# Strassen sums of h by GpSimd, the first pair's first product among the direct blocks, a PSUM copy queued ahead of a split

## The chip, the cores and the metric

The kernel runs on one core of a Trainium2 chip. The metric is the time of one execution on the device in microseconds; several executions are timed, and their median counts. Engines are named as in the profile: PE (TensorE), with PEld for its weight loads, DVE (VectorE), ACT (ScalarE), POOL (GpSimd) and SP, which issues the DMAs. Each engine works through its own queue of instructions in order; semaphores tie the queues together.

## What is computed

One layer of a hybrid network on 1024 latent tokens of width 1024, with 256 context tokens as a prefix. A token mixer (state space scan, Fourier mixing and pooling side by side) is followed by a ConvFFN, and the change lies in the second:

```python
def conv_ffn(h, w_up, conv_w, conv_b, w_down, grid):
    a = h @ w_up
    a = dwconv2d_grid(a, conv_w, conv_b) if grid else dwconv1d(a, conv_w[1], conv_b)
    val, gate = jnp.split(a, 2, axis=-1)
    return (jax.nn.gelu(gate) * val) @ w_down
...
x = post_norm(x, mix_lat, g1, ln1_g[l], ln1_b[l])
ffn_lat = conv_ffn(modulate(x, sh2, sc2), ffn_w_up[l], ffn_conv_w[l], ffn_conv_b[l], ffn_w_down[l], True)
x = post_norm(x, ffn_lat, g2, ln2_g[l], ln2_b[l])
```

`w_up` has 2 x 2816 columns: 22 pairs of a value block and a gate block, 128 channels each. The convolution is a 3x3 depthwise one over a grid 64 tokens wide. All is float32.

## The kernel before

Numbers are split into a high and a low half (`hi = round(x)`, `lo = x - hi`, written to tiles of type float32r), and a product is three matmuls: high by high, high by low, low by high. `split` writes the high half on ACT and the low half on POOL unless another engine is given. The modulated input of the ConvFFN, h, lies transposed in `h2h[q]` and `h2l[q]`: q is the half of the tokens (512 each), and the middle index is one of eight blocks of 128 features.

The up-projection runs over the 22 pairs. The first seven (`PS = 7`) are direct: blocks n = 0 to 13, each 48 matmuls over eight feature blocks into a PSUM tile of 128 x 1024 (line 1521). After every second feature block `slot()` runs a unit of the down-projection (`down_unit`), if there is one: six matmuls into `pdn`, an eviction on DVE that adds them to `xt` (lines 1190 and 1192), and a store to `x_scratch`. There are two `pdn` buffers, and three tiles of 128 x 1024 in PSUM. After its matmuls a block is convolved by `conv2d`: one ACT instruction for the centre tap (line 1212) and eight DVE instructions for the others (line 1234), which read PSUM and add in SBUF. `gated` applies GELU on ACT, the product on POOL (line 1475) and the split. `down_raw` loads a block of `w_down` and scales it on POOL (line 1449).

The other 15 pairs use a Strassen scheme on part of the product: feature blocks `K2..K2+2` and `K1..K1+2` (2 to 4 and 5 to 7), the two halves of the tokens, and the value and gate columns make a 2 x 2 by 2 x 2 block product with seven multiplications. It needs sums of blocks on both sides:

- On the side of h they are made once, by `combine(k)` for k = 0, 1, 2, in pairs 3 to 5 (lines 1283 to 1300). `whole` adds the two halves of a block of h to one float32 block (four times, line 1288), four differences follow (lines 1295 to 1298), and three splits write `Tt`. All of it runs on DVE but for the high halves on ACT. The call stands in `tc.issue_after(lastv[0].ins)`: the instructions of the block that run on the engine of that last convolution tap, DVE, are ordered behind it. The buffers `ta` and the first half of `tb` are used by each k in turn. `last_t4` (line 1302) then writes a fourth group of sums into blocks `K1..K1+2` of `h2h[1]` and `h2l[1]`, once block 13 has read them.
- On the side of the weights they are made for each pair by `pair_sums` (lines 1317 to 1333), from the raw value and gate blocks that `pair_raw` loads into two buffers: sums and differences on POOL (1325, 1326, 1329, 1332), splits by ACT and POOL into the tiles S1, S2 and S3. These lie in the memory of `ta`, `tb` and `t4r`.

`pair(i)` (line 1372) runs the matmuls of one pair, all in `mm` (line 1349). `first_product(i)` is 9 matmuls of the value block by h into X, half of a PSUM tile, and ACT copies X to the other half Z (line 1370). Then X goes on with more products; Z gets those with S2 and S1, and a product with S3 goes to a tile `p7`. The first product of a later pair is issued at the end of the pair before it; that of pair 7 at the start of its own. `pair_value` splits the value block, `pair_gate` the gate block.

Tile, the layer that the kernel is written in, decides the order of the instructions in every engine's queue beforehand, by a list of what is ready in a model of the time, and by the order of writing where several are. So the order on chip can differ from that of the code; `tc.issue_after` adds edges. `eng = cycle(V)` gives DVE each time, `G` is POOL, `V` DVE, `S` ACT, `TE` PE.

Of the kernel before, what the change touches and what calls it, by code (L numbers as in the profile page):

```python
# [8 lines left out]
F32 = mybir.dt.float32  # L9
F32R = mybir.dt.float32r  # L10
AF = mybir.ActivationFunctionType
ALU = mybir.AluOpType
# [21 lines left out]
def hybrid_layer(  # L34
# [6 lines left out]
    V, S, G, TE = nc.vector, nc.scalar, nc.gpsimd, nc.tensor  # L41
# [22 lines left out]
    def psa(name):  # L64
        return psx[-1].tile([P, 1024], F32, tag="A", name=name, bufs=psx[1])
# [5 lines left out]
    def qt(tag, name, shape=(P, 1024), dt=F32):  # L71
        return qp.tile(list(shape), dt, tag=tag, name=name)
# [30 lines left out]
    for i, src in enumerate((c, c_ctx, ssd_conv_w, ssd_conv_b, ssd_norm_w, pool_scale, b_ada[:, 0:2048])):  # L103
# [4 lines left out]
        n = v.shape[0]  # L108
# [99 lines left out]
    def cycle(*items):  # L208
        st = [-1]

        def nxt():
            st[0] += 1
            return items[st[0] % len(items)]
        return nxt

    def split(raw, hi, lo, eng=None):

        S.activation(hi, raw, AF.Identity)  # L218
        return (eng or G).tensor_tensor(lo, raw, hi.bitcast(F32), op=ALU.subtract)  # L219
# [435 lines left out]
    def pre(n):  # L655
        return [lambda a=pres.pop(0): chunk_pre(*a) for _ in range(min(n, len(pres)))]
# [370 lines left out]
    rest = pre(16)  # L1027
# [60 lines left out]
    h2h, h2l = [None, None], [None, None]  # L1088
# [37 lines left out]
    KS, PS, TS = 3, 7, 3  # L1126
# [121 lines left out]
    def slot():  # L1248
        if units:
            down_unit(units.pop(0))  # L1250
# [27 lines left out]
    eng = cycle(V)  # L1278

    def t4raw(k):  # L1280
        return t4r[:, k, :] if k < 2 else tb[:, 1, :]

    def combine(k):

        ta, b22 = qt("q5", f"ta{k}", [P, 2, 512]), tb[:, 0, :]

        def whole(dst, q, kt):
            eng().tensor_tensor(dst, h2h[q][:, kt, :].bitcast(F32), h2l[q][:, kt, :].bitcast(F32), op=ALU.add)

        b11, b12, b21 = ta[:, 0, :], ta[:, 1, :], t4raw(k)  # L1290
        whole(b11, 0, K1 + k)
        whole(b12, 1, K1 + k)
        whole(b22, 1, K2 + k)
        whole(b21, 0, K2 + k)
        eng().tensor_tensor(b11, b12, b11, op=ALU.subtract)
        eng().tensor_tensor(b12, b22, b12, op=ALU.subtract)
        eng().tensor_tensor(b22, b22, b11, op=ALU.subtract)
        eng().tensor_tensor(b21, b21, b22, op=ALU.subtract)
        for j, src in ((0, b11), (1, b22), (2, b12)):
            split(src, Tt[j][k][:, 0, :], Tt[j][k][:, 1, :], eng())  # L1300
# [16 lines left out]
    def pair_sums(i):  # L1317


        v, g = raws[i]  # L1320
        s1, s2, s3 = [qt(tag, f"S{j}_{i}", [P, 8, P], F32R) for j, tag in enumerate(STAG)]
        sw[i] = {j: [(t[:, k, :], t[:, 3 + k, :]) for k in range(KS)] for j, t in ((1, s1), (2, s2), (3, s3))}
        sw[i][4] = [(s1[:, 6, :], s3[:, 6, :]), (s1[:, 7, :], s3[:, 7, :]), (s2[:, 6, :], s2[:, 7, :])]
        a11, a12, a21, a22 = v[:, K1 : K1 + KS, :], v[:, K2 : K2 + KS, :], g[:, K1 : K1 + KS, :], g[:, K2 : K2 + KS, :]
        G.tensor_tensor(a21, a21, a22, op=ALU.add)
        G.tensor_tensor(a11, a21, a11, op=ALU.subtract)
        split(a11, s2[:, 0:3, :], s2[:, 3:6, :])
        split(a21, s1[:, 0:3, :], s1[:, 3:6, :])
        G.tensor_tensor(a12, a12, a11, op=ALU.subtract)
        split(a12[:, 0:2, :], s1[:, 6:8, :], s3[:, 6:8, :])  # L1330
        split(a12[:, 2:3, :], s2[:, 6:7, :], s2[:, 7:8, :])
        G.tensor_tensor(a11, a22, a11, op=ALU.subtract)
        split(a11, s3[:, 0:3, :], s3[:, 3:6, :])

    def pair_gate(i):

# [15 lines left out]
    def wk(w, k0, n=KS):  # L1352
        return [(w[0][:, k, :], w[1][:, k, :]) for k in range(k0, k0 + n)]

    def sk(i, j):
        return sw[i][j]
# [7 lines left out]
    pv, pq, zc = {}, {}, {}  # L1364

    def first_product(i):
        pv[i] = psa(f"pu{chan[2 * i]}")
        X, Z = pv[i][:, 0:512], pv[i][:, 512:1024]
        mm(X, wk(vw[i], K1), hk(0, K1), True)
        zc[i] = S.copy(Z, X)  # L1370

    def pair(i, mid):

        more = i + 1 < NPAIR
        if i not in pv:
            first_product(i)
        X, Z = pv[i][:, 0:512], pv[i][:, 512:1024]
        mm(X, wk(vw[i], K2), hk(0, K2))
        mm(X, wk(vw[i], 0, KD0), hk(0, 0, KD0))
        if more:  # L1380
            slot()
        mm(Z, sk(i, 2), tk(2))
        pq[i] = psa(f"pu{chan[2 * i + 1]}")
        Y, W_ = pq[i][:, 0:512], pq[i][:, 512:1024]
        S.copy(Y, Z)
        if more:
            slot()
        p7 = psb(f"p7_{i}")
        mm(p7, sk(i, 3), tk(3), True)
        s7 = post.tile([P, 512], F32, tag="s7", name=f"s7_{i}")  # L1390
        s7c = S.copy(s7, p7)
        if more:
            with tc.issue_after(s7c.ins):
                pair_value(i + 1)
            slot()
        mm(Z, sk(i, 1), tk(1))
        seed = seedw[0] = S.copy(W_, Z)
        with tc.issue_after(seed.ins):
            mid()
            down_split()  # L1400
        slot()

        def z_end():
            mm(Z, sk(i, 4), hk(1, K2))
            mm(Z, wk(vw[i], 0, KD0), hk(1, 0, KD0))

        if more:
            mm(Y, wk(gw[i], K2), hk(1, K1))
            slot()
            z_end()  # L1410
            slot()
        else:
            z_end()
        acc_v = conv2d(pv[i], chan[2 * i], [(0, 16)], off=None if more else (ring("ht2", "cu0"), ring("ht2", "cd0")))
        if more:
            with tc.issue_after(tap[0].ins):
                pair_sums(i + 1)
            if i + 2 < NPAIR:
                pair_raw(i + 2, 0)
            first_product(i + 1)  # L1420
            slot()
        else:
            mm(Y, wk(gw[i], K2), hk(1, K1))
        mm(Y, wk(gw[i], 0, KD0), hk(0, 0, KD0))
        if more:
            slot()
        mm(W_, wk(gw[i], 0, KD0), hk(1, 0, KD0))
        if more:
            with tc.issue_after(zc[i + 1].ins):
                pair_gate(i + 1)  # L1430
            if i + 2 < NPAIR:
                pair_raw(i + 2, 1)
        pqv = pq[i][:].rearrange("p (a n) -> p a n", a=2)
        V.tensor_tensor(pqv, pqv, s7.unsqueeze(1).broadcast_to([P, 2, 512]), op=ALU.add)
        return acc_v
# [66 lines left out]
    for i in range(NPAIR):  # L1502
        if i < PS:
            for n in (2 * i, 2 * i + 1):
                if n > 1 and n + 1 < 2 * PS:
                    wu[n + 1] = up_weights(n + 1)
                if n == 2 * PS - 1:
                    pair_raw(PS, 0)
                    pair_raw(PS, 1)
                    pair_value(PS)  # L1510
                ct = chan[n]
                w = wu.pop(n)
                if n < 3:
                    pt = first[n]
                    up_half(pt, w, 0)
                else:
                    pt = psa(f"pu{ct}")
                    for k in range(KD):
                        for j, (a, b) in enumerate(((w[0], h2h), (w[0], h2l), (w[1], h2h))):
                            for q in range(2):  # L1520
                                TE.matmul(pt[:, q * 512 : q * 512 + 512], a[:, k, :], b[q][:, k, :],  # L1521
                                          start=k == 0 and j == 0, stop=k == KD - 1 and j == 2)
                        if k % 2 == 1:
                            slot()
                acc = conv2d(pt, ct, [(0, 9)], begun) if n == 0 else conv2d(pt, ct, [(0, 16)])
                if n % 2 == 0:
                    acc_v = acc
            down_split()
            between(i)
            if TS <= i < TS + KS:  # L1530
                with tc.issue_after(lastv[0].ins):
                    combine(i - TS)
            if i == PS - 1:
                last_t4()
                pair_sums(PS)
                pair_raw(PS + 1, 0)
                pair_gate(PS)
                pair_raw(PS + 1, 1)
        else:
            acc_v = pair(i, lambda: between(i))  # L1540
            if i < NPAIR - 1:
                acc = conv2d(pq[i], chan[2 * i + 1], [(0, 16)])
            else:
                acc = conv2d(pq[i], chan[2 * i + 1], [(0, 8), (8, 16)], off=(qt("q3", "cu1"), qt("wl0", "cd1")), early=True)
        accs_[i] = acc_v, acc
# [165 lines left out]
```

## Time and profile before

| | |
|---|---|
| median of 3 runs | 1211.18 us (1209.03 to 1214.26) |
| the profiled execution | 1215.51 us |
| its span, first to last instruction | 1213.7 us |
| busy, share of the span: PE | 1130.9 us, 93% |
| PEld | 918.5 us, 76% |
| DVE | 991.2 us, 82% |
| POOL | 590.2 us, 49% |
| ACT | 459.9 us, 38% |
| granted clock of TensorE, mean | 0.981 |

A row of a timeline has the start in us, the length in us, the engine, the line, the operation, what it writes and reads, and how many instructions are merged in it; brackets give the idle time of that engine before it and what ended it. A row of waits has the engine and line, what it waited for, and then the total in us, the times and the longest. The ConvFFN begins at about 466 us, its units of the down-projection at 546, its Strassen pairs at 685; after 1141 comes the end of the down-projection with the last normalisation.

### The profile page before, as it was taken

The numbers are of one execution on the slowest core, as the hardware profiler recorded it, in microseconds if no ns is written. First come the engines' busy times: TensorE is split into PE (matmuls) and PEld (weight loads), VectorE is DVE, ScalarE is ACT, GpSimd is POOL, SyncE is SP. The second block draws the span as 40 slices with busy tenths as digits, with TensorE's granted clock in tenths as the row PEclk, the third lists the DMA queues.
The fourth block names the chain that finished last, engine by engine and source line by source line (L and its number), as shares of the span: only waits on it lengthen the run. The fifth ranks groups of instructions, "written<-read, shape, count | busy, mean of one in ns | idle before, by whom it ended". The sixth has DMA issues, their size and how long they took to land.

```text
span 1213.7 us, 15187 instructions
## 1 busy us (share of the span) xinstructions
PE 1130.9 (93%) x5328; PEld 918.5 (76%) x5328; DVE 991.2 (82%) x1407; ACT 459.9 (38%) x790; POOL 590.2 (49%) x470
## 2 busy tenths in 40 slices
PE   4899998889878998999999989999999999999986
PEld 2698887768756887788777768888888888888864
DVE  4788787688899889798999956877887787878866
ACT  2263566621444133342231333333333434333553
POOL 0010122244254024573465386767676767676756
PEclk9999999999989999999999999999999999999988
DMA  9849475557525314214545445555555565555513
GB/s 314 282 154 321 139 202 169 158 195 234 183 78 192 119 48 163 89 58 141 167 157 160 125 151 185 181 186 187 191 191 186 178 191 191 191 187 187 186 48 139
DMA packets 151875, 206.48 MB, mean 170 GB/s; under 512 B 12253, under 2 KB 89067, under 8 KB 151799
## 3 DMA queue, kind: packets, MB, share of 16 engines
q1 hardware_dynamic: 151799, 205.51, 52.4%
q8 instruction: 42, 0.69, 0.2%
q14 instruction: 34, 0.28, 0.1%
HBM read 148.76 MB, written 56.71 MB: 169 GB/s over the span
## 4 chain that ended last, share of the span: by engine, by line
PE 58%; DVE 17%; DMA 11%; POOL 4%; ACT 4%; issue 4%; SPq 1%; DVEq 0%; POOLq 0%; ACTq 0%
PE pu L1349 20%; PE pdn L1187 13%; PE pu L1521 6%; PE pout L1010 4%; DMA bc<-cs_scratch 3%; PE pl L1576 3%; PE pz L344 2%; PE p L1349 2%; PE px L445 2%; DVE cv L1234 2%; PE pu L1245 1%; DMA wa<-in_w_ada_dram 1%; DMA ctxr<-in_ctx_dram 1%; DMA wdr<-in_ffn_w_down_dram 1%; ACT EU L645 1%
## 5 line engine op out<-in xcount | busy, mean ns | idle before, releaser
L1234 DVE SCALAR_TENSOR_TENSOR cv<-pu,ffc,cv 128x945 f32<-128x945 f32 (+6 forms) x362 | 425.6, 1180 | 74.6 <-ACT cv L1212 64.9
L1187 PE MATMUL pdn<-wd,gh 128*128 128x512 f32 x576 | 182.2, 397 | 6.6 <-DVE xt L1190 6.1
L1187 PEld LDWEIGHTS pdn<-wd,gh 128*128 128x128 f32 x576 | 108.4, 189 | 33.4 <-DVE xt L1190 7.8
L1190 DVE TENSOR_TENSOR xt<-xt,pdn 128x512 f32<-128x512 f32 x128 | 87.3, 682 | 33.3 <-PE pdn L1187 28.2
L1187 PE MATMUL pdn<-wd,gl 128*128 128x512 f32 x288 | 114.1, 396 | 0.0
L219 POOL TENSOR_TENSOR wul<-wur,wuh 128x1024 fp32r<-128x1024 f32 x29 | 71.6, 2469 | 57.3 <-ACT wuh L218 42.4
L1449 POOL TENSOR_TENSOR wdr<-wdr,g2b 128x512 f32<-128x512 f32 x44 | 57.4, 1308 | 61.5 <-DMA wdr<-in_ffn_w_down_dram 61.5
L219 POOL TENSOR_TENSOR S<-wur,S 128x384 fp32r<-128x384 f32 (+2 forms) x75 | 62.1, 854 | 31.3 <-ACT S L218 30.6
L1212 ACT ACTIVATE cv<-pu,ffc 128x1024 f32<-128x1024 f32 (+3 forms) x46 | 53.5, 1165 | 43.8 <-PE pu L1349 22.1
L1475 POOL TENSOR_TENSOR cv<-cv,cv 128x512 f32<-128x512 f32 x44 | 58.6, 1351 | 22.2 <-ACT cv L1474 22.2
L1349 PE MATMUL pu<-T,S 128*128 128x512 f32 x270 | 67.1, 392 | 0.0
L644 POOL TENSOR_TENSOR bc<-bc,ncs 128x256 f32<-128x256 f32 x32 | 25.8, 810 | 79.4 <-DMA bc<-cs_scratch 68.7
L1187 PEld LDWEIGHTS pdn<-wd,gl 128*128 128x128 f32 x288 | 54.4, 189 | 12.9
L1349 PE MATMUL pu<-h2h,wuh 128*128 128x512 f32 x150 | 59.9, 400 | 3.4 <-ACT pu L1370 3.4
L219 POOL TENSOR_TENSOR gl<-cv,gh 128x512 fp32r<-128x512 f32 x44 | 57.2, 1320 | 10.9 <-ACT gh L218 10.0
L1474 ACT ACTIVATE cv<-cv 128x512 f32<-128x512 f32 x44 | 25.5, 626 | 91.8 <-DVE cv L1234 91.8
L1349 PEld LDWEIGHTS pu<-T,S 128*128 128x128 f32 x270 | 50.7, 188 | 11.6
L1349 PE MATMUL pu<-h2h,wul 128*128 128x512 f32 x150 | 59.5, 396 | 0.0
L1349 PE MATMUL pu<-h2l,wuh 128*128 128x512 f32 x150 | 59.2, 395 | 0.0
L206 POOL TENSOR_TENSOR h2l<-h2t,h2h 128x512 fp32r<-128x512 f32 x14 | 20.6, 1478 | 77.6 <-DVE h2h L205 77.6
L219 POOL TENSOR_TENSOR wd<-wdr,wd 128x512 fp32r<-128x512 f32 x42 | 53.7, 1301 | 4.4 <-ACT wd L218 4.2
L1521 PE MATMUL pu<-h2h,wuh 128*128 128x512 f32 x176 | 55.6, 397 | 0.0
(407 smaller groups left out, 2923.5 us busy)
## 6 DMA issues: line engine op xcount, KB each, us to landing
xt<-x_scratch SPq DMA_DIRECT2D x144, 256.0 KB
x_scratch<-xt SPq DMA_DIRECT2D x144, 256.0 KB
wur<-in_ffn_w_up_dram SPq DMA_DIRECT2D x44, 512.0 KB
wad<-in_w_ada_dram SPq DMA_DIRECT2D x32, 512.0 KB
wdr<-in_ffn_w_down_dram SPq DMA_DIRECT2D x44, 256.0 KB
wa<-in_w_ada_dram SPq DMA_DIRECT2D x32, 256.0 KB
bc<-cs_scratch SPq DMA_DIRECT2D x32, 256.0 KB
xr<-in_x_dram SPq DMA_DIRECT2D x8, 512.0 KB
```

The lines of the kernel that those rows point to most:

```text
L219: return (eng or G).tensor_tensor(lo, raw, hi.bitcast(F32), op=ALU.subtract)
L644: G.tensor_tensor(bc[:, 1], bc[:, 1], ncs[:, ch, b : b + 2].unsqueeze(2).broadcast_to([P, 2, P]), op=ALU.add)
L1010: TE.matmul(pt[:, nb * 512 : nb * 512 + 512], u, v[:, nb * 512 : nb * 512 + 512], start=first and i == 0, stop=last and i == 2)
L1187: TE.matmul(pt, u_, wd[nb][:, v_, :], start=i == 0, stop=i == n - 1)
L1190: V.tensor_tensor(xt, xt, pt, op=ALU.add)
L1212: tap[0] = S.activation(acc[:, a * 64 : b * 64], pt[:, a * 64 : b * 64], AF.Identity, bias=ffc[:, 396 + ct : 397 + ct], scale=factor(0, 0))
L1234: last = V.scalar_tensor_tensor(dst, pv[:, r0 + dy : r1 + dy, c0 + dx : c1 + dx], factor(dy, dx), dst, op0=ALU.mult, op1=ALU.add)
L1349: TE.matmul(dst, a[k][u], b[k][w], start=start and k == 0 and j == 0, stop=k == n - 1 and j == 2, skip_group_check=True)
L1449: G.tensor_tensor(raw, raw, g2b[:, s], op=ALU.mult)
L1475: G.tensor_tensor(acc[:, s], acc[:, s], acc_v[:, s], op=ALU.mult)
L1521: TE.matmul(pt[:, q * 512 : q * 512 + 512], a[:, k, :], b[q][:, k, :], start=k == 0 and j == 0, stop=k == KD - 1 and j == 2)
L1576: TE.matmul(accs[t][nb], u_, wd[nb][:, v_, :], start=t < NHALF and m == 0 and i == 0, stop=m == NG - 1 and i == 2, skip_group_check=t >= N ...
```

## The change

```diff
@@ combine(k)
         def whole(dst, q, kt):
-            eng().tensor_tensor(dst, h2h[q][:, kt, :].bitcast(F32), h2l[q][:, kt, :].bitcast(F32), op=ALU.add)
+            G.tensor_tensor(dst, h2h[q][:, kt, :].bitcast(F32), h2l[q][:, kt, :].bitcast(F32), op=ALU.add)
@@ pair_sums(i)
         G.tensor_tensor(a21, a21, a22, op=ALU.add)
         G.tensor_tensor(a11, a21, a11, op=ALU.subtract)
+        G.tensor_tensor(a12, a12, a11, op=ALU.subtract)
         split(a11, s2[:, 0:3, :], s2[:, 3:6, :])
         split(a21, s1[:, 0:3, :], s1[:, 3:6, :])
-        G.tensor_tensor(a12, a12, a11, op=ALU.subtract)
         split(a12[:, 0:2, :], s1[:, 6:8, :], s3[:, 6:8, :])
         split(a12[:, 2:3, :], s2[:, 6:7, :], s2[:, 7:8, :])
-        G.tensor_tensor(a11, a22, a11, op=ALU.subtract)
-        split(a11, s3[:, 0:3, :], s3[:, 3:6, :])
+
+        def rest():
+            G.tensor_tensor(a11, a22, a11, op=ALU.subtract)
+            split(a11, s3[:, 0:3, :], s3[:, 3:6, :])
+
+        return rest
@@ pair(i, mid)
             with tc.issue_after(tap[0].ins):
-                pair_sums(i + 1)
+                rest = pair_sums(i + 1)
+            first_product(i + 1)
+            with tc.issue_after(zc[i + 1].ins):
+                rest()
             if i + 2 < NPAIR:
                 pair_raw(i + 2, 0)
-            first_product(i + 1)
             slot()
@@ the direct blocks
                         if k % 2 == 1:
                             slot()
+                        if k == 5 and n == 2 * PS - 1:
+                            first_product(PS)
@@ the end of the direct blocks
                 last_t4()
-                pair_sums(PS)
+                pair_sums(PS)()
                 pair_raw(PS + 1, 0)
```

Four things differ. The 12 sums of line 1288 go from DVE to POOL. In `pair_sums` the a12 difference is written ahead of the first two splits. The last difference and its split, into S3, become `rest`; from pair 8 on it is written after the first product of the pair and its PSUM copy `zc`, and its ACT instruction is ordered behind that copy, while for pair 7 it follows at once. And the first product of pair 7 is written inside block 13, after the sixth of its eight feature blocks and the unit there. The number of matmuls and of sums is the same.

## The prediction

> **What bounds the kernel now.** I read the busy time of each engine in stretches of 15 us first, then what TensorE waits for, then the engines' timelines around each wait, since a share over the whole span mixes stages.
>
> ```profile
> span 1213.7 us, 15187 instructions
> 665.00:680.00 15.00, 10.34 (x39) 8.24 (x38) 14.93 (x15) 3.74 (x7) 7.26 (x5) 0.89 0.31 98
> 710.00:725.00 15.00, 11.56 (x49) 9.08 (x48) 12.04 (x12) 5.55 (x11) 12.77 (x13) 0.98 0.34 105
> 740.00:755.00 15.00, 15.00 (x67) 12.18 (x66) 9.98 (x11) 5.20 (x11) 10.59 (x11) 1.00 0.42 141
> PE pdn L1187 <- DVE xt L1190: 6.1, 4, 4.7
> PE pu L1349 <- ACT pu L1370: 3.4, 1, 3.4
> ```
>
> The columns of a stretch are its bounds and length, then busy time of PE, PEld, DVE, ACT and POOL, the granted clock, the DMA share. PE is full from 740 on (15.00 of 15.00), so there only PE work counts. Before it stand two holes, both where the direct blocks hand over to the Strassen pairs, and both in code that the change touches. The two rows below the stretches (PE's waits from 500 to 740) name them: one wait of 4.7 us on an eviction by DVE, one of 3.4 us on the PSUM copy at L1370.
>
> The first hole, on PE, then DVE, then POOL:
>
> ```profile
> 662.16 0.63 PE L1521 MATMUL pu<-h2h,wuh 128*128 128x512 f32 x2
> 664.50 0.62 PE L1521 MATMUL pu<-h2h,wul 128*128 128x512 f32 x2
> 669.77 1.22 PE L1187 MATMUL pdn<-wd,gh 128*128 128x512 f32 x2 [4.66 <-DVE xt L1190]
> 675.59 0.62 PE L1187 MATMUL pdn<-wd,gh 128*128 128x512 f32 x2
> 660.07 2.91 DVE L1288 TENSOR_TENSOR ta<-h2h,h2l 128x512 f32<-128x512 f32 x2
> 662.91 3.47 DVE L1288 TENSOR_TENSOR tb<-h2h,h2l 128x512 f32<-128x512 f32 x2
> 666.30 2.82 DVE L1295 TENSOR_TENSOR ta<-ta 128x512 f32<-128x512 f32 x1
> 669.04 0.67 DVE L1190 TENSOR_TENSOR xt<-xt,pdn 128x512 f32<-128x512 f32 x1
> 674.27 0.68 DVE L219 TENSOR_TENSOR T<-ta,T 128x512 fp32r<-128x512 f32 x1
> 674.88 1.19 DVE L1234 SCALAR_TENSOR_TENSOR cv<-pu,ffc,cv 128x945 f32<-128x945 f32 x1
> 659.42 3.01 POOL L1449 TENSOR_TENSOR wdr<-wdr,g2b 128x512 f32<-128x512 f32 x2
> 662.39 3.43 POOL L1475 TENSOR_TENSOR cv<-cv,cv 128x512 f32<-128x512 f32 x2
> 665.79 2.79 POOL L219 TENSOR_TENSOR wul<-wur,wuh 128x1024 fp32r<-128x1024 f32 x1
> ```
>
> Ten matmuls lie between the starts 662.16 and 664.50: 0.234 us each. The next was due at 664.50 + 2 x 0.234 = 664.97 and came at 669.77: **4.80 us**. The 18 matmuls from there to 675.59 took 5.82 instead of 4.21, at a lower clock: **1.61 us** more. The hole costs 6.41 us. It is DVE's order: the eviction that PE needs stands behind five sums of combine(2). A sum takes 0.60 us from start to start when alone (674.27 to 674.88), but the four L1288 took 666.30 - 660.07 = 6.23 us and the L1295 2.74, just while POOL ran one two-input operation after another. Each of the two engines waits here for the other.
>
> The second hole, on PE, ACT, POOL:
>
> ```profile
> 719.74 0.40 PE L1349 MATMUL pu<-h2h,gwl 128*128 128x512 f32 x1
> 723.58 0.51 PE L1349 MATMUL pu<-h2h,wuh 128*128 128x512 f32 x1 [3.44 <-ACT pu L1370]
> 728.73 0.62 PE L1187 MATMUL pdn<-wd,gh 128*128 128x512 f32 x2
> 722.51 0.52 ACT L218 ACTIVATE S<-wur 128x384 fp32r<-128x384 f32 x1 [8.84 <-POOL wur L1332]
> 722.94 0.58 ACT L1370 COPY pu<-pu 128x512 f32<-128x512 f32 x1
> 717.17 1.30 POOL L1449 TENSOR_TENSOR wdr<-wdr,g2b 128x512 f32<-128x512 f32 x1 [1.56 <-DMA wdr<-in_ffn_w_down_dram]
> 718.43 3.09 POOL L219 TENSOR_TENSOR S<-wur,S 128x384 fp32r<-128x384 f32 x4
> 721.48 0.99 POOL L1332 TENSOR_TENSOR wur<-wur,wur 128x384 f32<-128x384 f32 x1
> 723.11 1.01 POOL L219 TENSOR_TENSOR S<-wur,S 128x384 fp32r<-128x384 f32 x1 [0.63 <-ACT S L218]
> ```
>
> Due at 719.97, PE went on at 723.58: 3.61 us; its next 15 matmuls took 5.15 instead of 3.51, 1.64 more. Together **5.25 us**. The copy itself (0.58) had nothing to wait for but its place in ACT's queue: the S split ahead of it waited 8.84 us for POOL's L1332, which stood behind four split halves, a multiply and that multiply's DMA.
>
> **The change part by part.**
>
> *Copy ahead of the last split.* The L1332 difference and its split come into rest(), and the split is queued on ACT behind the copy. Nothing is added. The copy then needs only the first product, which PE finished before the 12 gate matmuls that end at 719.97 and two units of six, 24 x 0.234 = 5.6 us earlier. So the 5.25 us go. What is late next: the second product of this pair reads S2, due 15 matmuls and one unit of six after 719.97, at 719.97 + 21 x 0.234 = 724.9; POOL has all four halves by 721.5, 3.4 us before. The third product reads S3, due 15 matmuls later, at 728.4; its low half ended at 724.12, 4.3 us before. POOL's chain moves with PE, since the GELU ahead of it is queued behind a PSUM copy. Gain **5.3**; least, if these two margins are eaten and more, 2. In the other 13 pairs PE has no hole; swapping two ACT steps of 0.5 us there costs nothing as long as these margins cover it, and 0.5 a pair if not. The earlier a12 difference on POOL changes nothing: it ran ahead of the splits already.
>
> *Sums on GpSimd.* DVE loses 12 sums, POOL gets 12. POOL's price, and the gaps that could take them:
>
> ```profile
> L219 POOL TENSOR_TENSOR wd<-wdr,wd 128x512 fp32r<-128x512 f32 x42 | 53.7, 1301 | 4.4 <-ACT wd L218 4.2
> 610.09 2.41 POOL L219 TENSOR_TENSOR wul<-wur,wuh 128x1024 fp32r<-128x1024 f32 x1 [14.75 <-PE pdn L1187]
> 644.93 2.41 POOL L219 TENSOR_TENSOR wul<-wur,wuh 128x1024 fp32r<-128x1024 f32 x1 [11.15 <-ACT wuh L218]
> 656.91 1.02 POOL L1325 TENSOR_TENSOR wur<-wur 128x384 f32<-128x384 f32 x1 [7.05 <-DMA wur<-in_ffn_w_up_dram]
> ```
>
> POOL pays 12 x 1.30 = 15.6 us, 5.2 a combine. The L1325 row tells where they will stand: it is written after block 13 (line 1535), yet runs at 656.91, before block 13's matmuls (662.16). The scheduler puts work of POOL where POOL is free. The edge on the last convolution tap binds DVE's instructions alone. combine(1) and combine(2) can sum as soon as the combine before has let go of its two buffers, and right there are POOL's gaps of 14.75 and 11.15 us; DVE then runs taps that read PSUM, at 1.2 us each (674.88, with POOL starting an operation beside it). So I cost them at nothing there; without that cover it is the slower rival below.
>
> What DVE saves in a combine is bounded both ways: 4 x 0.60 = 2.4 us if the waits on POOL pass to the seven operations that stay, 6.2 if they go. [...] For the third combine a start earlier by what DVE lags counts too:
>
> ```profile
> 644.75 1.19 ACT L1212 ACTIVATE cv<-pu,ffc 128x1024 f32<-128x1024 f32 x1
> 649.20 3.69 DVE L1234 SCALAR_TENSOR_TENSOR cv<-pu,ffc,cv 128x945 f32<-128x945 f32 x3
> ```
>
> Convolution 11 could start at 645.9 and starts at 649.20. Two combines shorter by at least 2.4 each take these 3.3 us away, so combine(2) starts 3.3 earlier. With all waits still in it the eviction then falls at 665.7 and PE resumes at 666.5: 1.5 us of hole and no long low clock, a gain of 4.9. Without the sums ahead of it the hole goes whole: 6.4. I take **5.6**, the middle, since wul and L1449 stay where they are. The other three evictions that PE waited for (6.1 - 4.7 = 1.4 us) are the same thing in small; I take half, **0.7**, between 0 and 1.4.
>
> One cost: sums of combine(0) that read only the second token half can start while DVE still works at the norms that hold up PE:
>
> ```profile
> 464.14 2.48 DVE L1080 SCALAR_TENSOR_TENSOR xa<-xa,pn_mv,ln1g 128x1024 f32<-128x1024 f32 x1
> 475.95 1.27 DVE L1080 SCALAR_TENSOR_TENSOR xa<-xa,pn_mv,ln1g 128x1024 f32<-128x1024 f32 x1
> ```
>
> A meeting with POOL costs such an operation 1.2 us, and two sums qualify: 0 to 2.4, I take **0.6**, half a meeting.
>
> *First product earlier.* Nine matmuls (2.1 us) move ahead of block 13's last 12; PE's work stays. But last_t4 may only overwrite h2h[1] after these 12, and S2 waits for last_t4:
>
> ```profile
> 683.49 0.62 PE L1521 MATMUL pu<-h2h,wul 128*128 128x512 f32 x2
> 686.29 0.62 ACT L218 ACTIVATE h2h<-tb 128x512 fp32r<-128x512 f32 x1
> 689.44 1.05 DVE L219 TENSOR_TENSOR h2l<-tb,h2h 128x512 fp32r<-128x512 f32 x1
> 692.32 2.25 PE L1349 MATMUL pu<-T,S 128*128 128x512 f32 x9
> ```
>
> From block 13's last matmuls to the product that reads S2 are 8.8 us now, 6.7 then. 2.5 us of the present chain are DVE's backlog (the h2l at 689.44 comes that long after its h2h ends); that shrinks as DVE gets ahead. Bounds 0 and 2.1; I take **1.0**, as ends this far apart have no row nearer to one.
>
> **Sum:** 5.3 + 5.6 + 0.7 - 0.6 - 1.0 = 10.0 us off. Against the profiled execution (1215.51 us, span 1213.7 and 1.8 around it) that is 1205.5; the median shown is 4.3 us lower, 1211.18, and the forecast from it is **1201**. From 740 on nothing absorbs it, as PE is full.
>
> **Rivals.**
>
> *One hole stays* (the eviction keeps its place behind all seven operations, or the copy's hole returns as a wait on S2 or S3). For it: POOL is 12.77 of 15 us busy around 715. Against: the margins of 3.4 and 4.3 us. Gain 3.5 to 7, about 1206.
>
> *Returned at the handover:* the S2 chain keeps its 8 us, PE arrives there 6 us sooner plus 2.1, and the gain of the first hole comes back as a wait there, with S3 behind it late as well. For it: DVE's order in that place is fixed beforehand. Against: the rest of the chain starts from PE's own matmuls, and DVE's part shrinks with its backlog. Gain 0 to 4, about 1209.
>
> *POOL's queue in front of DVE (slower):* the sums stand where they stood, behind L1449 and L1475. They then begin at 665.79 and end 5.2 later, at 671.0; DVE, whose L1295 began at 666.30, stands 4.7 us longer, with evictions and taps queued behind it. Three combines: 14.1, less 5.3, is 8.8 slower: 1220. It decides from the point where two combines sum after their convolution's last tap. [...]
>
> **How the numbers follow.** Forecast 0.56; one hole stays 0.22; returned 0.10; POOL's queue 0.12. A measurement of this kernel tells about 0.5% (6.1 us, 1205.1) from no change. Half of the second case lies beyond it: faster 0.56 + 0.11 = 0.67. Same: 0.11 + 0.10 + 0.02 of the last (one combine only) = 0.23; slower 0.10. The range begins at the best ends (6.4 + 1.4 + 5.3 = 13.1, so 1198) less 1.5 for the spread of runs, 1196.5; it takes in the second case and most of the third: up to 1210.
>
> **What would show it.** PE's waits: no L1370 row and no eviction over 2 us near 665; L1288 rows on POOL in its gaps around 600 and 635, at 1.3 us; convolution 11 starting within 1.5 us of its ACT step; any wait ahead of the first T,S product under 2 us. Wrong, if L1288 rows on POOL start after a convolution's last tap with DVE idle at L1295, if PE waits there for S, or if PE has new holes after 740.

## The result and the profile after

| | before | changed |
|---|---|---|
| median | 1210.66 us (4 runs, 1209.03 to 1214.26) | 1202.12 us (4 runs, 1199.98 to 1204.77) |
| ratio to before, 95% interval | | 0.9923 [0.9896, 0.9950] |
| the profiled execution, its span | 1215.51, 1213.7 us | 1204.77, 1202.9 us |
| granted clock of TensorE, mean | 0.981 | 0.981 |

The kernel became 8.5 us faster by the medians; the forecast was 1201 us. One run of the kernel before that took 3799.59 us stands in the median of the last batch below (1212.91 us, 11 runs), but not in its ratios. The page of the changed kernel, its span:

```profile
span 1202.9 us, 15202 instructions
```

The same stretches as before, with the same columns (bounds, length, busy time of PE, PEld, DVE, ACT, POOL, granted clock, DMA share, GB/s):

```profile
665.00:680.00 15.00, 14.66 (x64) 11.49 (x63) 14.86 (x15) 3.02 (x6) 4.86 (x4) 1.00 0.33 102
...
710.00:725.00 15.00, 14.57 (x64) 11.55 (x63) 13.16 (x14) 3.86 (x6) 10.89 (x11) 1.00 0.56 185
725.00:740.00 15.00, 15.00 (x67) 12.23 (x66) 10.22 (x12) 5.81 (x10) 10.53 (x9) 1.00 0.67 218
```

And what PE waits for from 500 to 750, whole:

```profile
PE p L1353 <- DVE xt L1190: 0.4, 1, 0.4
PE pu L1353 <- POOL S L219: 0.4, 1, 0.4
PE pdn L1187 <- DVE xt L1190: 0.3, 1, 0.3
PE pu L1245 <- DVE h2l L206: 0.2, 1, 0.2
```

PE is now busy 14.66 us of the 15 in which it had 10.34, at the full clock (1.00, where it had 0.89), and the two rows of 4.7 and 3.4 us are gone; nothing of half a microsecond has taken their place. After 740 PE's waits are the same in both kernels, 4.9 and 0.8 us at `pl`, so no new hole came there. Lines of the code moved a little: L1349 of before is L1353, L1370 is L1374, L1332 is L1334, L1475 is L1481, L1521 is L1527.

Where the first hole was, timeline of the changed kernel on ACT, DVE, POOL and PE:

```profile
644.92 1.19 ACT L1212 ACTIVATE cv<-pu,ffc 128x1024 f32<-128x1024 f32 x1
646.41 3.69 DVE L1234 SCALAR_TENSOR_TENSOR cv<-pu,ffc,cv 128x945 f32<-128x945 f32 x3
657.29 1.07 DVE L1295 TENSOR_TENSOR ta<-ta 128x512 f32<-128x512 f32 x1
658.35 0.69 DVE L1190 TENSOR_TENSOR xt<-xt,pdn 128x512 f32<-128x512 f32 x1
658.96 1.12 DVE L1296 TENSOR_TENSOR ta<-tb,ta 128x512 f32<-128x512 f32 x1
...
663.40 2.90 DVE L219 TENSOR_TENSOR T<-ta,T 128x512 fp32r<-128x512 f32 x1
...
669.07 0.68 DVE L1190 TENSOR_TENSOR xt<-xt,pdn 128x512 f32<-128x512 f32 x1
662.89 2.86 POOL L219 TENSOR_TENSOR wul<-wur,wuh 128x1024 fp32r<-128x1024 f32 x1
630.92 1.70 POOL L1288 TENSOR_TENSOR ta<-h2h,h2l 128x512 f32<-128x512 f32 x1 [1.23 <-DVE T L219]
635.40 1.30 POOL L1288 TENSOR_TENSOR ta<-h2h,h2l 128x512 f32<-128x512 f32 x1
636.67 1.31 POOL L1288 TENSOR_TENSOR tb<-h2h,h2l 128x512 f32<-128x512 f32 x1
669.80 0.72 PE L1187 MATMUL pdn<-wd,gh 128*128 128x512 f32 x2 [0.34 <-DVE xt L1190]
```

Four things are to be seen. Three of the four sums of combine(2) ran on POOL between 631 and 638, 19 us ahead of its differences. Convolution 11 starts 1.49 us after its step on ACT, 4.45 before. The waits of DVE on POOL are still there: the split at 663.40 takes 2.90 us beside POOL's `wul`, where the one at 674.27 before took 0.68, and the seven operations that are left take from 657.29 to 669.07. The eviction between L1295 and L1296 stands behind one operation of the combine instead of five. The next one came three operations later before; now it stands behind all the other six, 10.1 us from 658.96 to 669.07, and PE waits 0.34 us for it.

Where the second hole was, timeline of the changed kernel on ACT, POOL and PE:

```profile
708.55 0.57 ACT L1374 COPY pu<-pu 128x512 f32<-128x512 f32 x1 [0.73 <-PE pu L1353]
717.49 0.53 ACT L218 ACTIVATE S<-wur 128x384 fp32r<-128x384 f32 x1 [8.36 <-POOL wur L1334]
716.43 1.02 POOL L1334 TENSOR_TENSOR wur<-wur,wur 128x384 f32<-128x384 f32 x1
713.68 0.39 PE L1353 MATMUL pu<-h2h,gwl 128*128 128x512 f32 x1
713.91 0.39 PE L1353 MATMUL pu<-h2h,wuh 128*128 128x512 f32 x1
```

The copy now waits for PE alone, 5 us before it is needed. The split that stood ahead of it waits for POOL as long as ever, 8.36 us, with nothing of PE behind it.

### The profile page after: what moved, and what is told of

It is laid out like the page before. It is cut to its first block, busy times and chain, and to the rows that moved or that the text cites. A ratio compares the mean times of both kernels' runs of the same rounds, so it can differ in the third digit from the quotient of the medians.

```text
span 1202.9 us, 15202 instructions
## 1 busy us (share of the span) xinstructions
PE 1129.9 (94%) x5328; PEld 918.1 (76%) x5328; DVE 984.6 (82%) x1395; ACT 461.1 (38%) x790; POOL 609.5 (51%) x482
## 4 chain that ended last, share of the span: by engine, by line
PE 69%; DVE 16%; DMA 6%; issue 3%; ACT 3%; POOL 2%; SPq 0%; DVEq 0%; ACTq 0%; POOLq 0%
PE pu L1353 22%; PE pdn L1187 16%; PE pu L1527 9%; PE pout L1010 4%; PE px L445 4%; PE pz L344 4%; PE pl L1584 3%; PE p L1353 3%; DMA bc<-cs_scratch 2%; DVE cv L1234 1%; PE pu L1245 1%; POOL cv L1224 1%; DMA xr<-in_x_dram 1%; DMA zb_r<-in_w_in_dram 1%; PE pm L298 1%
## 5 line engine op out<-in xcount | busy, mean ns | idle before, releaser
L1481 POOL TENSOR_TENSOR cv<-cv,cv 128x512 f32<-128x512 f32 x44 | 57.9, 1336 | 27.7 <-ACT cv L1480 27.7
L1353 PE MATMUL pu<-T,S 128*128 128x512 f32 x270 | 67.5, 393 | 0.4 <-POOL S L219 0.4
L1353 PEld LDWEIGHTS pu<-T,S 128*128 128x128 f32 x270 | 50.5, 188 | 12.8 <-POOL S L219 0.8
L1353 PE MATMUL pu<-h2h,wuh 128*128 128x512 f32 x150 | 59.1, 394 | 0.0
L206 POOL TENSOR_TENSOR h2l<-h2t,h2h 128x512 fp32r<-128x512 f32 x14 | 20.5, 1475 | 75.9 <-DVE h2h L205 75.9
L1353 PE MATMUL pu<-h2h,wul 128*128 128x512 f32 x150 | 59.0, 393 | 0.0
L1353 PE MATMUL pu<-h2l,wuh 128*128 128x512 f32 x150 | 58.5, 390 | 0.0
L1527 PE MATMUL pu<-h2h,wuh 128*128 128x512 f32 x176 | 55.3, 395 | 0.0
```

Source lines behind the costliest of these rows:

```text
L1353: TE.matmul(dst, a[k][u], b[k][w], start=start and k == 0 and j == 0, stop=k == n - 1 and j == 2, skip_group_check=True)
L1481: G.tensor_tensor(acc[:, s], acc[:, s], acc_v[:, s], op=ALU.mult)
```

## The experiments

Eleven runs were made. Spans can't be compared whole: the stages ahead of the ConvFFN, which no edit touches, end up to 5.9 us apart from one profiled execution to the next (the last run of `pout` matmuls starts at 465.95 in the changed kernel, at 460.07 without the sums). So the starts of PE's matmuls cut each profiled execution in stages. The rows for stage B are quoted with the experiments; this one of before goes with the 692.32 row above:

```profile
545.88 0.63 PE L1187 MATMUL pdn<-wd,gh 128*128 128x512 f32 x2
```

```
A: from the last run of pout matmuls to the first unit of the down-projection (pdn)
B: from there to the first product of T and S (all of blocks 6 to 13: the first hole)
C: from there to the first pl matmul (the pairs: the second hole)
                      A        B        C
before              80.45   146.44   448.13
changed             82.24   138.64   442.89
changed, again      81.45   138.96   443.42
sums alone          81.29   139.11   449.45
copy alone          81.56   145.15   444.05
first product alone 80.56   146.09   448.97
no first product    82.33   139.93   443.68
sums held back      81.83   139.27   443.93
sums behind taps    80.48   162.19   443.82
no sums             80.47   146.29   443.77
cut                 82.40   137.79   443.66
cut, sums on DVE    80.46   142.14   444.04
no sums, cut        81.58   137.79   443.35
```

**One part at a time.** The theory was that of the prediction, two holes with a cause each; the rival, that one of them stays or comes back at the handover. Three kernels took one part of the change each, a fourth all but the first product.

```diff
# sums alone: before, with
-            eng().tensor_tensor(dst, h2h[q]..., h2l[q]..., op=ALU.add)
+            G.tensor_tensor(dst, h2h[q]..., h2l[q]..., op=ALU.add)
# copy alone: the changed kernel with this line, and the next two, undone
# first product alone: before, with
+                        if k == 5 and n == 2 * PS - 1:
+                            first_product(PS)
# no first product: the changed kernel without these two lines
```

> The kernel before with the 12 sums on POOL and nothing else. My theory: the hole of 6.4 us ahead of the eviction and the small eviction waits go (about 8 us together), the front loses 1.8 us where sums meet the last norms, and the hole of 5.3 us at the PSUM copy stays: about 6 us faster, 1204.5, with a wait of 3 to 4 us on the copy L1370 in PE's list. Rival A, the copy's hole is a sequel of the first one: then it goes too, about 11 us faster. Rival B, it is the earlier first product that gives DVE the time: then the eviction's hole stays, under 2 us.

> The kernel before with the last difference and split of the weight sums behind the PSUM copy (and the a12 difference earlier), the sums of h still on DVE and the first product of pair 7 at its old place. My theory: the copy's hole goes, 5.3 us, the eviction's hole of 6.4 us stays: about 1205.5. Rival: the split and its difference, now late, return the hole as a wait on S3: no change.

> The kernel before with the first product of pair 7 inside block 13 and nothing else. My theory: it gives nothing; the product waits for nothing in either place, and the 2.1 us by which the way from block 13's last matmuls to the first product with S2 gets shorter show as a wait there, 0 to 2 us slower, since DVE's backlog is unchanged. Rival: DVE catches up while PE does the nine matmuls, and the eviction's hole of 4.8 us shrinks by up to 2.

> The changed kernel with the first product of pair 7 back at its old place. My theory: the wait of 0.4 us and the halt around it at the first product with S2 (0.9 us in all) go, all else stays: 0 to 1 us faster than the changed kernel, about 1201.5. Rival: the move is a needed part of the change, and without it PE stands 1 to 3 us somewhere between block 13 and pair 7 (for the copy L1370, or for an eviction).

Measured against before (1213.02 us, 25 runs): sums alone 1209.37 us, 0.9963 [0.9948, 0.9978]; copy alone 1209.56, 0.9968 [0.9953, 0.9984]; first product alone 1215.28, 1.0015 [0.9997, 1.0032]; all but the first product 1201.77, 0.9908 [0.9889, 0.9927]. The longest of PE's waits with the sums alone, and where it waits in the second hole:

```profile
PE pu L1349 <- ACT pu L1370: 4.3, 1, 4.3
```

```profile
547.24 0.63 PE L1187 MATMUL pdn<-wd,gh 128*128 128x512 f32 x2
686.35 0.73 PE L1349 MATMUL pu<-T,S 128*128 128x512 f32 x2
716.32 0.99 POOL L1332 TENSOR_TENSOR wur<-wur,wur 128x384 f32<-128x384 f32 x1
718.41 0.79 PE L1349 MATMUL pu<-h2h,wuh 128*128 128x512 f32 x1 [4.29 <-ACT pu L1370]
```

The longest with the copy alone:

```profile
PE pdn L1187 <- DVE xt L1190: 4.5, 4, 3.0
```

So each part closes its own hole and leaves most of the other. The sums take 7.3 us off stage B (146.44 to 139.11), the copy 4.1 off stage C (448.13 to 444.05). Both gained less than I had expected, 6 and 5.3 us, by medians 3.7 and 3.5; with the intervals neither expectation is excluded. In the stages the two parts help each other a little: with the sums alone PE is due at the copy 5.8 us earlier (718.41 - 4.29 = 714.1 against 719.97), POOL's L1332 only 5.2 (716.32 against 721.48), and the wait there grows from 3.4 to 4.3 us, so stage C gives 1.3 us back (449.45). That is a gain returned later, in small, though at the copy and not at S2, where the rival had it: the wait for S is 0.4 us. It ends where the copy no longer waits for POOL. Not all of it need be the sums': with the first product alone the wait at the copy is 4.6 us (and none at S2, where I had expected one), though stage B is as long there as before. The first product gives nothing that can be measured over the whole, alone or taken away. In stage B the changed kernel is 1.0 to 1.3 us shorter with it than without (138.64 and 138.96 against 139.93): without it PE waits 1.6 us for an eviction at 668, with it 0.3 and 0.6. The rival for this run had 1 to 3 us; but the sums alone, without the move as well, have only 0.8 us there, so the move is not shown to be the reason.

**Sums held back, sums put behind the taps, no sums.** Is the collision at the front the price of the sums on POOL, what would they cost in the queue that the slower rival named, and what would their absence bring?

```diff
# sums held back: the changed kernel, all of combine behind a weight split of block 4
+                    if n + 1 == 4:
+                        held[0] = anchor[0]
...
-                with tc.issue_after(lastv[0].ins):
+                with tc.issue_after(lastv[0].ins), tc.issue_after(held[0].ins):
# sums behind taps: a multiply on POOL reads the convolution just ended, the sums follow it
+        mark = G.tensor_tensor(tick, acc[:, 512:1024], g2b[:, 0:512], op=ALU.mult)
...
+            with tc.issue_after(mark.ins):
+                G.tensor_tensor(dst, ...)
# no sums: whole() is not called, and the differences read the high halves
+        eng().tensor_tensor(b11, h12, h11, op=ALU.subtract)
```

> The changed kernel once more, to stand on the same chip beside the next three: 1202 on a chip where the kernel before takes 1210.7, that is 0.992 of it.

> The changed kernel, where the sums of the first combine are ordered behind the weight split of block 4 on POOL, so that they no longer run between 459 and 504 us. My theory: they met norms and the last splits of h there and cost 1.8 us; held back they run at 512 to 560 us beside taps that read PSUM: 1.8 us faster than the changed kernel, 0.990 of the time before, and the first unit of the down-projection 1.8 us earlier against the eviction at 439. Rival: the later start of that unit is the order of PE (transposes behind more matmuls), not the sums: then under 0.5 us.

> The changed kernel, where each combine first multiplies half of the convolution that has just ended by a constant on POOL (a result that nothing reads) and its four sums are ordered behind that: the rival by which sums stand behind the last tap. My price for it was 4.7 us a combine against the kernel before, 14.1 in all, less 5.3 for the copy: about 1220, 1.007 of the time before, with DVE idle at L1295 (6 us or more) in all three combines and PE waiting for evictions in all three. If the place of the sums does not matter, it stays at the changed kernel's 1202 or a little over (three multiplies, 3.9 us of POOL).

> The changed kernel without the 12 sums: the differences read the high halves in place of the sums, so the low halves of those blocks are left out of the Strassen part. It is the floor of what any place for the sums can give. My theory: beyond the front (1.8 us) the sums cost next to nothing on POOL: 2 to 3 us faster than the changed kernel, about as the kernel with the first combine held. Rival: the sums on POOL still hold up POOL's other work or the combines: 4 us or more faster.

Against before (1212.48 us, 17 runs): the changed kernel again 1201.77 us, 0.9918 [0.9901, 0.9934]; sums held back 1201.24, 0.9912 [0.9897, 0.9928]; sums behind the taps 1223.8, 1.0096 [1.0080, 1.0112]; no sums 1205.41, 0.9955 [0.9931, 0.9978].

Held back, the sums spare PE 0.4 us at the front (the section on the prediction has the rows) and cost it a wait for a weight split instead; over the whole the kernel is not to be told from the changed one. The 1.8 us that I had expected did not come. One of PE's waits there:

```profile
PE pu L1530 <- POOL wul L219: 1.0, 1, 1.0
```

Behind the taps the sums stand where the slower rival had them. The longest of DVE's waits from 540 to 700 in that kernel, then of PE's from 540 to 750:

```profile
DVE ta L1298 <- POOL ta L1291: 9.9, 3, 5.3
```

```profile
PE pdn L1187 <- DVE xt L1190: 14.8, 2, 8.6
PE pdn L1187 <- DVE xt L1192: 3.5, 1, 3.5
```

The rival had DVE stand 4.7 us in each combine and priced the kernel 8.8 us above before; DVE stands 9.9 in three, at most 5.3, and the medians differ by 1223.8 - 1212.48 = 11.3 us. Stage B is 15.8 us longer than before (162.19 against 146.44), where the rival had 14.1: PE waits 18.3 us for evictions, against 6.5 before. The mechanism was right, and the size nearly. In the changed kernel it did not come, since the scheduler put the sums where POOL was free.

The kernel without the sums was to be the limit of what moving them can bring, 2 to 3 us faster than the changed kernel; its median is 3.6 us slower. Its twelve runs scatter from 1201.2 to 1211.9 us and the two intervals just overlap, so the trace has to tell it. Stage B takes 146.29 us, as long as before, though DVE has 12 operations less and POOL none more. Its timeline, the third combine on DVE, and PE:

```profile
540.54 0.63 PE L1187 MATMUL pdn<-wd,gh 128*128 128x512 f32 x2
...
653.98 0.85 DVE L1292 TENSOR_TENSOR ta<-h2h,h2h 128x512 f32<-128x512 f32 x1
...
662.19 1.47 DVE L219 TENSOR_TENSOR T<-ta,T 128x512 fp32r<-128x512 f32 x1
663.59 1.27 DVE L1190 TENSOR_TENSOR xt<-xt,pdn 128x512 f32<-128x512 f32 x2
664.31 1.22 PE L1187 MATMUL pdn<-wd,gh 128*128 128x512 f32 x2 [2.36 <-DVE xt L1190]
...
686.83 2.48 PE L1350 MATMUL pu<-T,S 128*128 128x512 f32 x9
```

All seven operations stand in one row of 9.6 us, and two evictions ("x2") behind them. PE can go two units ahead, one for each buffer, and then waits: 2.36 us here, 6.2 in the three combines. Before, the first of the two stood behind five of eleven operations; in the changed kernel it stands behind one of seven. The rival that one hole stays had named this: the eviction that keeps to the end of all seven operations.

**Is it the order or the load?** That left two theories. *Order*: what counts is how much stands between two evictions. *Load*: DVE had 12 operations too many. Three kernels cut a combine in four groups, each behind one more eviction; one of them leaves the sums on DVE, one has none.

```diff
# cut: the changed kernel, with
+        def c1():
+            eng().tensor_tensor(b12, b22, b12, op=ALU.subtract)
+            cut(0, b11)
...
+        later.extend((lambda: None, lambda: None, c1, c2, c3))
...
                             slot()
+                            if later:
+                                with tc.issue_after(evict[0].ins):
+                                    later.pop(0)()
# cut, sums on DVE: the same on the copy alone (so without the early first product);
#   two of the four sums go with c1 and c3
# no sums, cut: the same on the kernel without the sums
```

> The changed kernel with the seven VectorE operations of a combine cut into four groups, each behind one more eviction of a down unit (one operation, then two, two and two, the last groups in the next block), instead of seven in nearly one row. Theory 'order' (TensorE waited because two evictions stood behind all the sums of a combine; what counts is where the evictions stand, not how much VectorE has to do): the eviction waits of the changed kernel (0.6 and 0.7 us in the 440-to-750 stretch) fall below 0.5 us together; from the first down unit to the first product of T and S 138 to 138.7 us (138.6 to 139.0 in the changed kernel); 0 to 1 us faster than it, ratio to before 0.990 to 0.992. Theory 'load' (TensorE waited because VectorE had 12 operations too many): no gain over the changed kernel either, 138.6 to 139.5, and the evictions behind the later groups may wait 1 us.

> The kernel with the copy ahead of the last split alone, sums still on VectorE, and its eleven operations of a combine cut into groups of three, three, three and two behind one eviction each. 'Order': the eviction waits (4.5 us in four there, 146.4 and 145.2 us from the first down unit to the first product of T and S in the kernel before and with the copy alone) go to 1.5 us or less, the stage takes 138.5 to 140.5 us, ratio to before 0.990 to 0.9935: cutting the row does what moving the sums did. 'Load': VectorE is as far behind as before (convolution 11 starts over 3 us after its first step on ScalarE), the waits move to later evictions or to the products of T and S, stage 143 to 146 us, ratio 0.9955 to 0.998.

> The kernel without the 12 sums (differences read the high halves, the low halves of those blocks are left out), its seven operations of a combine cut into four groups behind one eviction each. Without the cut it had 6.2 us of eviction waits and 146.3 us from the first down unit to the first product of T and S. 'Order': the waits fall below 1 us, the stage takes 138 to 139 us, ratio to before 0.988 to 0.992. 'Load' or anything else that the missing sums changed: waits over 3 us stay, stage 144 to 147 us, ratio 0.994 to 0.997.

Against before (1212.91 us, 11 runs): cut 1201.14 us, 0.9905 [0.9888, 0.9922]; cut with the sums on DVE 1204.29, 0.9931 [0.9914, 0.9947]; cut without sums 1201.49, 0.9901 [0.9877, 0.9925]. Stage B of each, cut first, then cut with the sums on DVE, then cut without sums:

```profile
544.29 0.62 PE L1188 MATMUL pdn<-wd,gh 128*128 128x512 f32 x2
682.08 2.48 PE L1365 MATMUL pu<-T,S 128*128 128x512 f32 x9
```

```profile
544.58 0.63 PE L1188 MATMUL pdn<-wd,gh 128*128 128x512 f32 x2
686.72 0.74 PE L1365 MATMUL pu<-T,S 128*128 128x512 f32 x2 [0.48 <-ACT S L218]
```

```profile
544.37 0.63 PE L1188 MATMUL pdn<-wd,gh 128*128 128x512 f32 x2
682.16 2.46 PE L1362 MATMUL pu<-T,S 128*128 128x512 f32 x9
```

The order theory holds for the kernel without sums: the same operations, cut, take stage B from 146.29 to 137.79 us and leave no wait on an eviction there. Alone it is a part of the answer. With the sums still on DVE the cut takes stage B from 145.15 us in the copy alone, from which it was made, to 142.14. Moving the sums instead takes it to 139.93 (the changed kernel without the first product, which this kernel lacks too): 3.0 against 5.2 us. I had expected 138.5 to 140.5 by *order* and 143 to 146 by *load*, and it came between. What is left there are 3.1 us of waits for evictions, two of them, later ones; the longer (timeline, PE):

```profile
642.46 0.74 PE L1188 MATMUL pdn<-wd,gh 128*128 128x512 f32 x2 [1.69 <-DVE xt L1191]
```

Between that eviction and the one ahead of it stand four taps and the last group, now of three operations. So both count: how much a combine has to do, and where the evictions stand in it. Cut with the sums on POOL and cut without any sums have the same stage B, 137.79 us: the sums on POOL cost stage B nothing. The cut kernel is the fastest by its median, with two waits of 0.6 us left in the whole stretch, but its interval and that of the changed kernel overlap: it isn't told apart from it.

## Why the prediction was right

**The bound** was read right: two holes, each with a cause of its own. Sums alone leaves the second (4.3 us), copy alone most of the first (4.5 us of eviction waits), the changed kernel has neither. The rival that one hole stays fell with that, though each half of the change alone would have been it.

**The copy, 5.3 us.** Stage C is 5.2 and 4.7 us shorter in two executions of the changed kernel, 4.1 in the one of the copy alone. Mechanism and size hold: the copy waits for PE only, and the products with S2 and S3 cost pair 8 no wait, as the margins of 3.4 and 4.3 us had it.

**The sums, 5.6 + 0.7 us.** Stage B is 7.3 us shorter with the sums alone; of the changed kernel's 7.8, 1.0 to 1.3 go with the first product. The working held in its parts: combine(2) starts 3.0 us sooner behind convolution 11's step on ACT (3.3 were counted), the waits on POOL stayed with the seven operations, near the lower of the two bounds (11.8 us from the first to the last where 14.8 had been), and the hole went whole because no sum stands ahead of the eviction. What the step took for given is that the eviction keeps its place when operations go. In the kernel without sums it did not, and there the same 12 operations less are worth nothing in stage B. The prediction had that order among its rivals, but no row that decides between the two, so it was luck that the eviction came where the step needed it. Why the scheduler orders the two kernels differently is not shown; that the order decides is shown by the cut.

**The front, -0.6 us.** The term was about right, the trace at first reads worse. Stage A is 1.8 us longer in the changed kernel. Timeline of PE before, in the changed kernel, and in the copy alone, where no sum runs on POOL, at a hole ahead of the last transposes of h:

```profile
482.50 1.12 PE L189 MATMUL h<-ident,xn 128*128 128x128 f32 x4 [3.48 <-ACT h2t L200]
...
484.98 0.69 PE L1245 MATMUL pu<-h2h,wul 128*128 128x512 f32 x1
485.50 0.40 PE L1245 MATMUL pu<-h2h,wuh 128*128 128x512 f32 x1
```

```profile
483.46 1.12 PE L189 MATMUL h<-ident,xn 128*128 128x128 f32 x4 [3.74 <-ACT h2t L200]
...
488.64 0.63 PE L1245 MATMUL pu<-h2h,wul 128*128 128x512 f32 x1
```

```profile
480.63 1.11 PE L189 MATMUL h<-ident,xn 128*128 128x128 f32 x4 [3.31 <-ACT h2t L200]
...
486.24 0.60 PE L1245 MATMUL pu<-h2h,wuh 128*128 128x512 f32 x1
```

The hole is 3.7 to 3.8 us wherever sums run early on POOL, 3.3 to 3.5 elsewhere, the held sums among them: about 0.4 us is the collision. The hole's end comes 17.07 us after the last `pout` run before and 17.51 after, the same 0.4. Of the two sums that run there early, one met a two-input norm: L1081 at 459.44 takes 2.40 us where it took 1.28 before, and L1080 after it takes 1.78 instead of 2.48. Of the rest of the 1.8, 1.2 is the low clock behind the hole: it lasts 2.5 us before (482.50 to 484.98) and 5.2 in the changed kernel, and PE is at the next transposes after 7.2 and 8.4 us. With the copy alone it lasts 5.6, so it is not the sums'.

**The first product, -1.0 us**, is not borne out. The wait for S that was feared is 0.4 us in the changed kernel, and as much without the move, and stage B is shorter with the move, not longer. The times alone would not exclude the 1.0 us: 1.0015 [0.9997, 1.0032] alone reaches from 0.4 us faster to 3.9 slower.

**The sum**: 10.0 predicted; 0.9923 of 1210.66 is 9.3 us, and the interval reaches from 6.1 to 12.6. By their ratios the two halves alone bring 4.5 and 3.9 us. By stages the profiled execution gains 7.8 + 5.2 - 1.8 = 11.2. The sum came near partly by luck: the low clock at the front, 1.2 us, was not in it, and the first product's term has the other sign in stage B.

**The slower rival** had nearly the right price and the wrong condition, as the experiment behind the taps shows. Its point of decision, sums after the last tap, is met by no combine of the changed kernel. A sum takes 1.31 us on POOL (636.67) against 0.68 for the shortest one on DVE before, and still costs stage B nothing here.

## What to carry to other kernels

When an in-order engine holds another one up, count what stands between two of the instructions that the other waits for, not what the engine has to do in all: here four operations less in a row of eleven did nothing where the evictions went behind the other seven, and a cut of the row alone did more than half of the work (3.0 of 5.2 us) with no operation less. An operation about twice as slow on another engine (1.31 us on POOL against 0.68 on DVE) cost next to nothing here where that engine would have waited, and made the kernel 11.3 us slower where its queue put it last; look for what in the profile decides between the two. Where two holes follow each other, closing the first alone can widen the second (4.3 us of wait at the copy with the sums alone, 3.4 before): cost the edits together, and compare by stages when the stages ahead scatter by as much as the effect.

## What the runs showed of the hardware

*The same hole, two prices.* Behind the hole at the front PE's matmuls run at the low clock (0.63 us for a record, 0.40 later) for 2.5 us before and for 5.2 to 5.6 us in the changed kernel and in the copy alone, though the three holes are 3.5, 3.7 and 3.3 us long. Over 16 us around it the granted clock is 0.89 before and 0.79 in the other two. The kernel with the sums alone has the same hole as the changed one, 3.74 us, and the low clock for only 3.4 us. From the hole's end to the next transposes PE takes 7.1 to 7.4 us in seven of twelve kernels, one profiled execution each, and 8.4 to 8.6 in the other five, among them two kernels without a sum on POOL: 1.2 us that come and go. The prediction took what followed a hole (1.6 us in both) as a part of the hole; by these rows it does not follow from the hole's length. What sets it instead, no run here shows.

*A cast beside POOL.* Timeline of the changed kernel, POOL and DVE, and of before, DVE:

```profile
496.41 1.31 POOL L1288 TENSOR_TENSOR t4r<-h2h,h2l 128x512 f32<-128x512 f32 x1 [0.99 <-DVE h2l L206]
496.51 1.49 DVE L205 CAST h2h<-h2t 128x512 fp32r<-128x512 f32 x1 [0.23 <-ACT h2t L200]
```

```profile
494.63 0.43 DVE L205 CAST h2h<-h2t 128x512 fp32r<-128x512 f32 x1 [0.24 <-ACT h2t L200]
```

An operation with one input, 0.43 us alone, took 1.49 while a sum ran on POOL; before, the one at 483.40 took 1.42 beside the 1.30 us L206 that POOL began at 483.23. The prediction looked for such meetings only among the two-input norms; a cast belongs in that list.
